# A transformer block's late modulation sums: half parts, a ring of three weight buffers, and Pool's queue

## The chip, the cores and the metric

The kernel runs on one core of a Trainium2 chip. The core has five engines that work side by side, each through its own instructions in a fixed order: TensorE (PE, with its weight loads shown as PEld), VectorE (DVE), ScalarE (ACT), GpSimd (POOL) and SyncE (SP), which only issues transfers. [...] The metric is the device time of one execution in microseconds (us), lower being better. All data is float32.

## The reference, cut to what matters

One layer of a hybrid diffusion block over 1024 tokens of width 1024, with 256 context tokens. A vector `c` gives six modulation vectors: `mod = silu(c) @ w_ada + b_ada`, split into shift, scale and gate for the mixers (parts 0, 1, 2) and for the feed-forward part (3, 4, 5).

```python
mod = jax.nn.silu(c) @ w_ada[i] + b_ada[i]
sh1, sc1, g1, sh2, sc2, g2 = jnp.split(mod[:, None, :], N_MOD, axis=-1)
h = modulate(rmsnorm(x, norm1_g[i]), sh1, sc1)
q, k, v, hv, hx1, hx2, gna, ghy = jnp.split(h @ w_in[i], IN_SPLITS, axis=-1)
y_na = neighbourhood_attention(q, k, v, k_c, v_c, na_rpb[i])    # with 256 context keys
y_hy = hyena_mixer(hv, hx1, hx2, *hy_params)
x = x + g1 * gated_merge(gna, ghy, y_na, y_hy, w_na_o[i], w_hy_o[i], w_out[i])
h2 = modulate(rmsnorm(x, norm2_g[i]), sh2, sc2)
x = x + g2 * swiglu(h2, ffn_w1[i], ffn_w3[i], ffn_w2[i])
return rmsnorm(x, final_g)
```

The Hyena mixer convolves over all tokens with long filters. A filter is a small network of the position (64 hidden units, then `w3`) times an exponential decay, and the convolution is done by Fourier transforms: `irfft(rfft(u) * rfft(filter))`, for two orders and 512 channels. The filters depend on parameters only, not on `x`.

## The kernel before, in words

**Stages.** After the first norm the kernel holds the modulated tokens (`hT`, split into two halves of precision, `hTh` and `hTl`) in SBUF. `project` multiplies them by 40 column chunks of `w_in`, three matrix products for each pair of tiles (`in_ps`, L194); chunks 4 to 11 also multiply the context (`ctx_ps`). Results are evacuated from PSUM by ScalarE (`proj`), for some chunks turned to token order on TensorE (`tm_ps`) and copied by ScalarE (`tm`, L554, two buffers, one PSUM bank `psc`), and stored to scratch memory by DMAs on Pool's queue (`qk`, `kc`, `vtok`, `vctok`, `z`, `hx`, L555, L606 and L618). The weights of the next chunk are loaded on SP (`wr`, L180) and split by ScalarE (`wh`) and VectorE (`wl`).

**Beside the projection** runs the generator `side()`: first the filters' spectra merged with the late modulation's sums, then four convolutions (order 0 and 1, each for two halves of the channels). `_merged` sets the order of the program: it draws from each generator by the units that it yields against its weight, filters 97 and sums 39, and `side` 460 against 39 chunks of projection. The program order decides the order on every engine; the framework below adds the semaphores.

**`filters`** (L335 on) works in four blocks, one for each order and half of the channels. In a block, TensorE computes 8 tiles of raw filter (`filt_ps`, L349), VectorE multiplies each by its decay tile `dec` (L353, result `fv`), which SP loads (L346) into two buffers. Then VectorE does three levels of butterflies (`fx`, `x`, `b`, `a`, L361 to L413), and TensorE multiplies the 8 results `a` by transform matrices `matf`, loaded on SP (`dft_ps`, L425 to L427). ScalarE copies each `dft_ps` to `ks` (L372, three buffers), and SP stores it to scratch memory as a spectrum (L373), which a convolution reads later (L453). `filt_ps` and `dft_ps` share a ring of five PSUM banks, `psf`.

**`ada_sums`** (L843 on) computes modulation parts 2 to 5 without TensorE. For each part VectorE clears an accumulator of 128 x 1024 (`aacc`, L848), SP copies the bias into its first row (L849), and in eight steps SP loads 128 rows of `w_ada` (`wal`, 512 KB, L852) and VectorE adds them, each row times its element of `silu(c)` (L853). `wal` and `aacc` have one buffer each. The accumulator is stored to scratch memory on Pool's queue (L855). Much later `ada_late` (L857 on) reads the four accumulators and adds their 128 rows up on TensorE.

**The pool** `filt` that holds these tiles is closed when filters and sums are done, and the convolutions' tiles take its place in SBUF.

Of the kernel before, what the change touches and what calls it, by code (L numbers as in the profile page):

```python
# [10 lines left out]
F32 = mybir.dt.float32  # L11
F32R = mybir.dt.float32r
AF = mybir.ActivationFunctionType
ALU = mybir.AluOpType
# [4 lines left out]
P = 128  # L19
D = 1024  # L20
# [138 lines left out]
class Block:  # L159
# [176 lines left out]
    def filters(self, pool, psf, hid, w3):  # L336

        nc, a = self.nc, self.a
        for hf in range(2):
            for o in range(2):  # L340
                v = [pool.tile([P, 4, 2, 256], F32, tag="v8", name="fv") for _ in range(2)]
                c0 = o * 512 + hf * 256
                for n2 in range(0, 8, 2):
                    for j in range(2):
                        dec = pool.tile([P, 512], F32, tag="dec", name="dec", bufs=2)
                        nc.sync.dma_start(dec, a["decay"][hf, n2 // 2, j])  # L346
                        ps = psf.tile([P, 512], F32, tag="f", name="filt_ps")
                        for n in range(2):
                            nc.tensor.matmul(ps[:, n * 256:(n + 1) * 256],  # L349
                                             hid[64 * j:64 * j + 64, (n2 + n) * P:(n2 + n + 1) * P],  # L350
                                             w3[64 * j:64 * j + 64, c0:c0 + 256], start=True, stop=True)
                        i = n2 % 4
                        nc.vector.tensor_tensor(v[n2 // 4][:, i:i + 2, j, :], ps.rearrange("p (n c) -> p n c", n=2),  # L353
                                                dec.rearrange("p (n c) -> p n c", n=2), op=ALU.mult)
                    yield 1.3
                b = pool.tile([1, 256], F32, tag="hb", name="hb", bufs=1)
                nc.sync.dma_start(b, a["hbias"][0:1, o, hf, :])
                nc.vector.scalar_tensor_tensor(v[0][0:1, 0, 0, :], b, 2.0 ** -10, v[0][0:1, 0, 0, :],
                                               op0=ALU.mult, op1=ALU.add)
                x = pool.tile([P, 4, 2, 256], F32, tag="v8", name="fx")  # L360
                nc.vector.tensor_add(x[:, :, 0, :], v[1][:, :, 0, :], v[1][:, :, 1, :])  # L361
                nc.vector.tensor_sub(x[:, :, 1, :], v[1][:, :, 1, :], v[1][:, :, 0, :])
                fl = lambda t: t.rearrange("p a b c -> p (a b c)")
                nc.vector.scalar_tensor_tensor(fl(v[1]), fl(x), S2, fl(v[0]), op0=ALU.mult, op1=ALU.add)
                yield 4.6
                nc.vector.scalar_tensor_tensor(fl(x), fl(x), -S2, fl(v[0]), op0=ALU.mult, op1=ALU.add)
                parts, spectra = self.forward(pool, psf, v[1], x)
                for ci in range(5):
                    if ci:
                        for j, us in enumerate(spectra()):  # L370
                            k = pool.tile([P, 512], F32, tag="ks", name="ks", bufs=3)
                            nc.scalar.copy(k, us)  # L372
                            nc.sync.dma_start(self.spec[o][hf][ci - 1][j], k)  # L373
                    if ci < 4:
                        parts()
                        yield 5.4 if ci % 2 == 0 else 1.9
# [466 lines left out]
    def ada_sums(self, pool):  # L843

        nc, a = self.nc, self.a
        for part in range(2, 6):
            acc = pool.tile([P, D], F32, tag="aacc", name="aacc", bufs=1)
            nc.vector.memset(acc, 0.0)  # L848
            nc.sync.dma_start(acc[0:1, :], a["b_ada"][0:1, part * D:(part + 1) * D])  # L849
            for k in range(8):  # L850
                w = pool.tile([P, D], F32, tag="wal", name="wal", bufs=1)
                nc.sync.dma_start(w, a["w_ada"][k, :, part * D:(part + 1) * D])  # L852
                nc.vector.scalar_tensor_tensor(acc, w, self.cs[:, 2 * k:2 * k + 1], acc, op0=ALU.mult, op1=ALU.add)  # L853
                yield 1.2
            nc.gpsimd.dma_start(self.accd[part], acc)  # L855

    def ada_late(self, pool, psf, gates):  # L857

# [578 lines left out]
```

## Time and profile before

| | |
|---|---|
| device time, median of 3 runs (lowest to highest) | 1757.57 us (1751.41 to 1759.25) |
| profiled execution: device time | 1752.59 us |
| profiled execution: span from first to last instruction | 1750.7 us |
| mean granted TensorE clock | 0.981 |
| TensorE busy | 1670.1 us (95% of the span) |
| VectorE busy | 1226.4 us (70%) |
| ScalarE busy | 662.8 us (38%) |
| Pool busy | 142.8 us (8%) |
| moved by DMA | 285.36 MB, 163 GB/s over the span |

The profile is one execution. A row of a group gives line, engine, operation, result and operands, count, busy time and mean duration, then idle time of the engine just before and what ended it ("<-" and the releaser). A row of waits gives who waited for whom: us in total, times, the longest. SPq is SP's DMA queue. A row of DMA issues gives the count, the size and the median time from issue to landing. In a row of a stretch stand its bounds and length, the busy time of each engine in the order PE, PEld, DVE, ACT, POOL (count of instructions in brackets), then the granted TensorE clock (1.00 is full), the DMA engines' mean busy share and GB/s.

### The profile page before, as it was taken

Reading aid. Unit: us, or ns where it says so; the run is one execution under the profiler, and the core shown is the slowest. Engines: PE = TensorE matmul, PEld = TensorE weight load, DVE = VectorE, ACT = ScalarE, POOL = GpSimd, SP = SyncE. Lnnn points to the kernel's source line nnn. Section 1 sums busy time; section 2 is a strip of 40 time slices with the busy share of each in tenths; the row PEclk is TensorE's granted clock in tenths of the full one; section 3 lists DMA queues with packets and bytes.
Section 4 is the critical chain, followed back from the end, with each engine's and each line's share of the span. In section 5 each row is a group of like instructions: output and inputs, shape, how many; then the busy total and the mean of one; then the engine's idle time right before and its main releaser. Section 6 shows DMA issues by size and latency. Waiting matters only on the chain.

```text
span 1750.7 us, 22516 instructions
## 1 busy us (share of the span) xinstructions
PE 1670.1 (95%) x8128; PEld 1324.1 (76%) x8128; DVE 1226.4 (70%) x2039; ACT 662.8 (38%) x1147; POOL 142.8 (8%) x250
## 2 busy tenths in 40 slices
PE   5999899999999998999998999999999999999997
PEld 2777676777777776787777787788888888878886
DVE  4586487799797865656865868887665656479467
ACT  4611222313221213546664215633343333344555
POOL 0000110101000004010300000001000001100000
PEclk8999999999999999999999999999999999999999
DMA  8375766655464428436757424243322322394344
GB/s 337 112 244 189 242 197 211 210 155 181 137 210 155 173 81 238 129 119 190 204 164 253 146 67 168 106 142 133 108 91 102 103 97 97 126 381 149 102 120 151
DMA packets 111469, 285.36 MB, mean 163 GB/s; under 512 B 14707, under 2 KB 23543, under 8 KB 109053
## 3 DMA queue, kind: packets, MB, share of 16 engines
q1 hardware_dynamic: 91888, 221.32, 38.6%
q0 software_dynamic: 18816, 62.14, 10.4%
q8 instruction: 65, 1.06, 0.3%
q10 hardware_dynamic: 653, 0.44, 0.1%
q14 instruction: 47, 0.39, 0.1%
HBM read 213.86 MB, written 69.99 MB: 162 GB/s over the span
## 4 chain that ended last, share of the span: by engine, by line
PE 50%; issue 27%; DVE 9%; DMA 9%; POOL 3%; ACT 2%; SPq 0%; POOLq 0%; DVEq 0%; ACTq 0%
PE in_ps L194 17%; PE dx_ps L1306 6%; PE out_ps L1086 5%; PE dft_ps L425 4%; PE dz_ps L1306 3%; DMA wal<-in_w_ada 2%; PE dft_ps L426 2%; PE dft_ps L427 2%; PE x_ps L1148 2%; PE dy_ps L1306 2%; POOL g L1259 1%; PE pt_ps L761 1%; PE na_ps L194 1%; DVE aacc L853 1%; DMA kraw<-qk 1%
## 5 line engine op out<-in xcount | busy, mean ns | idle before, releaser
L194 PE MATMUL in_ps<-hTh,wl 128*128 128x512 f32 x640 | 258.8, 405 | 6.4 <-ACT proj L596 6.2
L194 PE MATMUL in_ps<-hTh,wh 128*128 128x512 f32 x640 | 252.6, 395 | 0.0
L194 PE MATMUL in_ps<-hTl,wh 128*128 128x512 f32 x640 | 252.5, 395 | 0.0
L194 PEld LDWEIGHTS in_ps<-hTh,wl 128*128 128x128 f32 x640 | 121.5, 190 | 34.2 <-ACT proj L596 6.8
L194 PEld LDWEIGHTS in_ps<-hTh,wh 128*128 128x128 f32 x640 | 121.5, 190 | 26.4 <-issue 0.7
L194 PEld LDWEIGHTS in_ps<-hTl,wh 128*128 128x128 f32 x640 | 121.8, 190 | 25.6 <-issue 1.3
L175 DVE TENSOR_TENSOR ol<-ws,oh 128x512 fp32r<-128x512 f32 x88 | 60.2, 689 | 56.7 <-ACT oh L174 56.5
L174 ACT CAST wh<-wr 128x1024 fp32r<-128x1024 f32 x40 | 41.9, 1048 | 126.7 <-PE in_ps L194 102.5
L175 DVE TENSOR_TENSOR wl<-wr,wh 128x1024 fp32r<-128x1024 f32 x40 | 48.8, 1220 | 55.9 <-ACT wh L174 55.8
L175 DVE TENSOR_TENSOR ol<-ar,oh 128x512 fp32r<-128x512 f32 x77 | 53.0, 688 | 46.4 <-ACT oh L174 46.4
L174 ACT CAST oh<-ar 128x512 fp32r<-128x512 f32 x77 | 47.9, 621 | 82.5 <-PE dx_ps L1306 37.1
L425 PE MATMUL dft_ps<-a,matf 128*128 128x512 f32 x128 | 69.0, 622 | 9.1 <-DVE a L413 5.5
L174 ACT CAST oh<-ws 128x512 fp32r<-128x512 f32 x88 | 54.3, 622 | 48.4 <-PE x_ps L1148 16.8
L1306 PE MATMUL dx_ps<-ol,oh 128*128 128x512 f32 x176 | 69.7, 396 | 1.7 <-DVE ol L175 1.7
L1306 PE MATMUL dx_ps<-oh,ol 128*128 128x512 f32 x176 | 67.5, 392 | 3.9 <-ACT oh L174 3.6
L749 DVE CUSTOM_DVE_ANT_0 pe<-s_ps,bias 128x640 f32<-128x640 f32 x64 | 50.1, 820 | 29.1 <-PE s_ps L744 29.1
L750 ACT ACTIVATE pe<-pe,mx 128x640 f32<-128x640 f32 x64 | 52.6, 822 | 44.8 <-DVE mx L749 44.7
L1306 PE MATMUL dx_ps<-oh 128*128 128x512 f32 x176 | 69.3, 394 | 0.0
L853 DVE SCALAR_TENSOR_TENSOR aacc<-wal,cs,aacc 128x1024 f32<-128x1024 f32 x32 | 41.1, 1283 | 39.7 <-DMA wal<-in_w_ada 39.5
L175 DVE TENSOR_TENSOR ol<-wr,oh 128x512 fp32r<-128x512 f32 x70 | 48.1, 689 | 20.0 <-ACT oh L174 19.9
L174 ACT CAST oh<-wr 128x512 fp32r<-128x512 f32 x70 | 43.2, 621 | 50.0 <-PE y_ps L1148 18.2
L1088 DVE TENSOR_TENSOR x<-x,out_ps 128x512 f32<-128x512 f32 x64 | 43.2, 685 | 21.5 <-PE out_ps L1086 21.5
(392 smaller groups left out, 4234.2 us busy)
## 6 DMA issues: line engine op xcount, KB each, us to landing
wr<-in_w SPq DMA_DIRECT2D x50, 512.0 KB, 3.3
wr<-in_w_in SPq DMA_DIRECT2D x40, 512.0 KB, 4.5
ar<-g SPq DMA_DIRECT2D x77, 256.0 KB, 2.7
wal<-in_w_ada SPq DMA_DIRECT2D x32, 512.0 KB, 4.0
g<-t POOLq DMA_DIRECT2D x49, 256.0 KB, 3.0
matf<-in_dft_f SPq DMA_DIRECT2D x32, 384.0 KB, 4.6
bias<-in_rpb SPq DMA_DIRECT2D x64, 192.0 KB, 3.0
w<-in_w SPq DMA_DIRECT2D x44, 256.0 KB, 5.4
```

The source lines that it names most:

```text
L174: self.nc.scalar.copy(hi, src)
L175: self.nc.vector.tensor_sub(lo, src, hi.bitcast(F32))
L194: mm = nc.tensor.matmul(ps, ww[:, k * P:(k + 1) * P], xx[:, k, pos:pos + width], start=(i == 0), stop=(i == n - 1))
L425: nc.tensor.matmul(ps, m[:, 0], v.rearrange("p a b -> p (a b)"), start=True, stop=False)
L426: nc.tensor.matmul(ps[:, 0:256], m[:, 1], v[:, 1], start=False, stop=False)
L427: nc.tensor.matmul(ps[:, 256:512], m[:, 2], v[:, 0], start=False, stop=True)
L749: nc.vector.tensor_tensor_reduce(pe, ps[:, 256:896], bt, -1.0, 3e38, ALU.add, ALU.min, mx[:, 0:1])
L750: nc.scalar.activation(pe, pe, AF.Exp, bias=mx[:, 0:1], scale=-1.0, accum_out=mx[:, 1:2])
L853: nc.vector.scalar_tensor_tensor(acc, w, self.cs[:, 2 * k:2 * k + 1], acc, op0=ALU.mult, op1=ALU.add)
L1086: nc.tensor.matmul(ps, gg[x][:, tk], ww[y][:, sl], start=(i == 0), stop=(i == n - 1))
L1088: nc.vector.tensor_add(x1[:, sl], x1[:, sl], ps)
L1306: nc.tensor.matmul(ps[j], x[u][:, j * P:(j + 1) * P], w[v], start=(start and i == 0 and c == 0), stop=(stop and i == N - 1 and k == len(re ...
```

## The change

`ada_sums` is rewritten. The 4 parts x 8 steps become 4 parts x 2 halves x 8 steps, on tiles of 128 x 512. The weights are loaded by DMAs on Pool's queue, 256 KB each, into a ring of three buffers; the load of step n + 2 is written ahead of the sum of step n. The accumulator has two buffers; it is cleared by Pool in place of VectorE, and its bias row is copied on Pool's queue. Each half is stored on its own, on Pool's queue as before. A step yields 0.6 in place of 1.2, so that the sums weigh the same in the merge. Besides, the stores of the spectra move from SP's to Pool's queue, and the decay tiles have four buffers in place of two. The arithmetic is the same.

```diff
--- before.py
+++ after.py
@@ -342,7 +342,7 @@
                 c0 = o * 512 + hf * 256
                 for n2 in range(0, 8, 2):
                     for j in range(2):
-                        dec = pool.tile([P, 512], F32, tag="dec", name="dec", bufs=2)
+                        dec = pool.tile([P, 512], F32, tag="dec", name="dec", bufs=4)
                         nc.sync.dma_start(dec, a["decay"][hf, n2 // 2, j])
                         ps = psf.tile([P, 512], F32, tag="f", name="filt_ps")
                         for n in range(2):
@@ -370,7 +370,7 @@
                         for j, us in enumerate(spectra()):
                             k = pool.tile([P, 512], F32, tag="ks", name="ks", bufs=3)
                             nc.scalar.copy(k, us)
-                            nc.sync.dma_start(self.spec[o][hf][ci - 1][j], k)
+                            nc.gpsimd.dma_start(self.spec[o][hf][ci - 1][j], k)
                     if ci < 4:
                         parts()
                         yield 5.4 if ci % 2 == 0 else 1.9
@@ -843,16 +843,27 @@
     def ada_sums(self, pool):
 
         nc, a = self.nc, self.a
-        for part in range(2, 6):
-            acc = pool.tile([P, D], F32, tag="aacc", name="aacc", bufs=1)
-            nc.vector.memset(acc, 0.0)
-            nc.sync.dma_start(acc[0:1, :], a["b_ada"][0:1, part * D:(part + 1) * D])
-            for k in range(8):
-                w = pool.tile([P, D], F32, tag="wal", name="wal", bufs=1)
-                nc.sync.dma_start(w, a["w_ada"][k, :, part * D:(part + 1) * D])
-                nc.vector.scalar_tensor_tensor(acc, w, self.cs[:, 2 * k:2 * k + 1], acc, op0=ALU.mult, op1=ALU.add)
-                yield 1.2
-            nc.gpsimd.dma_start(self.accd[part], acc)
+        steps = [(part, h, k) for part in range(2, 6) for h in range(2) for k in range(8)]
+        cols = lambda part, h: slice(part * D + h * 512, part * D + h * 512 + 512)
+        ws = []
+
+        def load(part, h, k):
+            ws.append(pool.tile([P, 512], F32, tag="wal", name="wal", bufs=3))
+            nc.gpsimd.dma_start(ws[-1], a["w_ada"][k, :, cols(part, h)])
+
+        for step in steps[:2]:
+            load(*step)
+        for n, (part, h, k) in enumerate(steps):
+            if n + 2 < len(steps):
+                load(*steps[n + 2])
+            if k == 0:
+                acc = pool.tile([P, 512], F32, tag="aacc", name="aacc", bufs=2)
+                nc.gpsimd.memset(acc, 0.0)
+                nc.gpsimd.dma_start(acc[0:1, :], a["b_ada"][0:1, cols(part, h)])
+            nc.vector.scalar_tensor_tensor(acc, ws.pop(0), self.cs[:, 2 * k:2 * k + 1], acc, op0=ALU.mult, op1=ALU.add)
+            if k == 7:
+                nc.gpsimd.dma_start(self.accd[part][:, h * 512:(h + 1) * 512], acc)
+            yield 0.6
 
     def ada_late(self, pool, psf, gates):
```

## The prediction

> **What bounds the kernel now.** I read the page's busy times first, then busy time by stretch, to find the stage that the edited lines belong to.
>
> ```profile
> PE 1670.1 (95%) x8128; PEld 1324.1 (76%) x8128; DVE 1226.4 (70%) x2039; ACT 662.8 (38%) x1147; POOL 142.8 (8%) x250
> ```
> ```profile
> core 0: us, PE busy (x) PEld busy (x) DVE busy (x) ACT busy (x) POOL busy (x), PEclk, DMA share, GB/s
> 77.00:340.00 263.00, 245.90 (x1122) 188.60 (x1121) 180.68 (x229) 59.33 (x96) 20.39 (x30) 0.95 0.65 210
> 400.00:650.00 250.00, 249.56 (x1050) 191.98 (x1049) 202.23 (x339) 53.70 (x76) 15.03 (x24) 1.00 0.47 159
> ```
>
> TensorE is the bound: 95% of the span, and 249.56 of 250 us in the convolutions at 400 to 650. All edited code runs in the filter stage, 77 to 340 us. There TensorE idles 263.00 - 245.90 = 17.1 us, and its clock is 0.95 where the convolutions have 1.00. Those are full, so a microsecond won here reaches the end of the kernel. The idle time, from the timeline of TensorE, with the wait and its releaser in brackets:
>
> ```profile
> 120.26 1.10 PE L425 MATMUL dft_ps<-a,matf 128*128 128x512 f32 x2 [2.64 <-issue]
> 143.50 2.07 PE L349 MATMUL filt_ps<-fw,hid 64*128 64x256 f32 x4 [2.28 <-DVE fv L353]
> 172.44 1.10 PE L425 MATMUL dft_ps<-a,matf 128*128 128x512 f32 x2 [0.96 <-issue]
> 201.68 2.08 PE L425 MATMUL dft_ps<-a,matf 128*128 128x512 f32 x2 [3.14 <-DVE a L413]
> 215.37 1.13 PE L349 MATMUL filt_ps<-fw,hid 64*128 64x256 f32 x4 [1.99 <-DVE fv L353]
> 245.01 1.22 PE L425 MATMUL dft_ps<-a,matf 128*128 128x512 f32 x1 [1.72 <-DVE a L413]
> 281.08 2.07 PE L349 MATMUL filt_ps<-fw,hid 64*128 64x256 f32 x4 [3.65 <-DVE fv L353]
> ```
>
> Seven waits, 16.4 us, all before a matrix product whose operand (`a`, in the two rows that name only "issue" too) or whose freed PSUM bank (`fv`) comes from VectorE. After them the clock falls (stretches of 5 us; the granted clock stands before the DMA share):
>
> ```profile
> 140.00:145.00 5.00, 2.72 (x9) 1.83 (x8) 2.65 (x4) 0.00 (x0) 0.00 (x0) 0.76 0.92 313
> 145.00:150.00 5.00, 5.00 (x14) 3.58 (x13) 2.48 (x3) 0.59 (x1) 0.00 (x0) 0.56 0.62 198
> 200.00:205.00 5.00, 3.32 (x6) 2.02 (x7) 3.42 (x4) 0.20 (x1) 0.71 (x1) 0.56 0.77 219
> 205.00:210.00 5.00, 5.00 (x24) 3.33 (x23) 1.95 (x2) 1.17 (x2) 0.00 (x0) 0.75 0.86 307
> 245.00:250.00 5.00, 4.99 (x14) 3.09 (x15) 4.33 (x8) 1.07 (x2) 0.38 (x2) 0.66 0.51 159
> 280.00:285.00 5.00, 3.92 (x9) 2.70 (x10) 3.69 (x5) 0.00 (x0) 0.00 (x0) 0.50 0.65 215
> ```
>
> Busy time times what the clock lacks of 1 gives 0.65 + 2.2 + 1.46 + 1.25 + 1.70 + 1.96 = 9.2 us of work at a lowered clock that full speed would not have needed. The prize is therefore 16.4 + 9.2 = 26 us at most. [...] By a reading that counts idle time alone the prize would be 16.4.
>
> Why is VectorE late, when it is busy only 180.68 of 263 us? Its own waits in this stage:
>
> ```profile
> DVE aacc L853 <- DMA wal<-in_w_ada: 39.5, 18, 7.4
> DVE aacc L848 <- DMA acc<-aacc: 11.7, 3, 6.3
> DVE fv L353 <- DMA dec<-in_decay: 6.5, 5, 2.9
> ```
>
> 57.7 us, all three at tiles that the change gives more buffers. VectorE works in order, so a sum that waits for its weights holds `fv` and `a` behind it.
>
> **The change part by part.** First, the sum by halves. Before, 32 products over 1024 columns; after, 64 over 512, whose price is that of the 512-column product `a`. Four memsets leave VectorE.
>
> ```profile
> L853 DVE SCALAR_TENSOR_TENSOR aacc<-wal,cs,aacc x32: 1272/1284/1286, 86.8 to 319.1; 128x1024 f32<-128x1024 f32 x32
> L413 DVE SCALAR_TENSOR_TENSOR a<-x,b 128x512 f32<-128x512 f32 x32 | 21.5, 686 | 4.6 <-PE dft_ps L427 4.5
> L848 DVE MEMSET aacc<- 128x1024 f32 x4 | 3.6, 912 | 12.0 <-DMA acc<-aacc 11.7 <-DVE hcTl L175 0.3
> ```
>
> 64 x 0.686 = 43.9 against 32 x 1.284 = 41.1 is +2.8; minus 3.6 for the memsets, VectorE's work changes by -0.8 us: nothing.
>
> Second, the ring. Before, one `wal` buffer: load and sum alternate, and each load starts only when the sum ahead has read the buffer. After, the load of step n+2 is issued ahead of step n's sum and needs the buffer of step n-1. It has two steps to arrive. There are 64 steps between the first sum (86.8) and the last (319.1), so a step is 232 / 64 = 3.6 us and two are 7.2.
>
> ```profile
> wal<-in_w_ada SPq DMA_DIRECT2D x32, 512.0 KB, 4.0
> spec<-ks SPq DMA_DIRECT2D x32, 256.0 KB, 4.1
> g<-t POOLq DMA_DIRECT2D x49, 256.0 KB, 3.0
> hx<-tm POOLq DMA_DIRECT2D x16, 256.0 KB, 4.9
> ```
>
> 256 KB on Pool's queue land in 3.0 to 4.9 us (its own rows, other directions of copy); I take 4.5, since DMA is as busy here as beside `hx`. That leaves 7.2 - 4.5 = 2.7 us of slack, against none before. Bounds: loads always on time, 39.5 us of VectorE's waits go; loads late as often as before, none go.
>
> What that does at one stall, the last and longest, can be followed in VectorE's timeline:
>
> ```profile
> 274.07 0.69 DVE L353 TENSOR_TENSOR fv<-filt_ps,dec 128x512 f32<-128x512 f32 x1 [3.14 <-PE filt_ps L349]
> 275.14 0.67 DVE L353 TENSOR_TENSOR fv<-filt_ps,dec 128x512 f32<-128x512 f32 x1
> 277.36 1.28 DVE L853 SCALAR_TENSOR_TENSOR aacc<-wal,cs,aacc 128x1024 f32<-128x1024 f32 x1 [1.55 <-DMA wal<-in_w_ada]
> 280.33 1.36 DVE L353 TENSOR_TENSOR fv<-filt_ps,dec 128x512 f32<-128x512 f32 x2 [1.69 <-DMA dec<-in_decay]
> ```
>
> The third `fv` frees the bank TensorE waits for. It starts at 280.33; with neither wait it would follow 275.14 + 0.67 + 0.69 for a half sum = 276.5, and TensorE, which stopped at 281.08 - 3.65 = 277.43, would hardly stop. The waits ahead of the others work alike, and each `a` stall stands behind more VectorE waiting than its own 1 to 3 us. So with loads on time nearly all 26 us go.
>
> Third, four decay buffers: they remove the 6.5 us above (0 if the loads are late for another reason: the lower bound). They count in the same 26.
>
> Fourth, the accumulator: two buffers, so a new half need not wait for the store of the one before, 11.7 us of VectorE. But its memset, its bias row and its weights now stand in one queue. At each of the 8 starts Pool issues load n+2 (waiting for sum n-1), then the memset, then the bias copy, and sum n waits for that copy. The nearest prices:
>
> ```profile
> L1253 POOL DMA_DIRECT2D g<-t x27 | 14.6, 541 | 309.4 <-DVE t L1251 283.8 <-DVE ol L175 25.0
> masks.py:197 POOL MEMSET ident<- 128x128 f32 x1 | 0.2, 204 | 0.3 <-POOLq L1433 0.3
> aacc<-in_b_ada SPq DMA_DIRECT2D x4, 4.0 KB
> ```
>
> No row has a Pool memset of 128x512; between 0.2 (128x128) and 0.9 (VectorE's, twice as wide) I take 0.8, four times the first. Then 0.54 + 0.8 + 0.54 + about 2.5 for the landing (no time is shown for it; below the 3.0 of 256 KB, above 0) = 4.4 us after the previous sum, against a step of 3.6: some 1 us of VectorE at 8 places, 0 to 2 each. TensorE's share of VectorE's waits so far is 16.4 of 57.7, so this is worth 8 x 0.3 = 2 us with 0 to 5 as bounds.
>
> Fifth, Pool's queue. It gains 64 weight loads, 8 bias rows, 32 spectra and 4 more stores: 108 x 0.54 = 58 us, and 8 x 0.8 = 6; with 20.4 now it is 85 of 263 us. Time is there; order is the question. A weight load now stands behind stores that wait for ScalarE:
>
> ```profile
> POOL vtok L555 <- ACT tm L554: 88.1, 8, 42.3
> POOL z L555 <- ACT tm L554: 64.4, 8, 27.8
> POOL vctok L555 <- ACT tm L554: 11.3, 4, 5.1
> ACT ks L372 <- PE dft_ps L427: 39.0, 23, 5.3
> SPq L373 <- ACT ks L372: 39.9, 24, 8.8
> SPq L852 <- DVE aacc L853: 36.3, 24, 3.8
> ```
>
> The 39.9 us in which SP stood before spectra now stand in Pool's queue; the copy they wait for comes up to 5.3 us after ScalarE is ready, more than the slack of 2.7. So some sums will still be late. Upper bound: all of the prize; lower bound 0; I take a quarter, 6 us. SP loses what held it, 36.3 us before weight loads and 39.9 before spectra, and its decay, DFT and projection weights come no later than now; no gain is counted for it, because no TensorE wait names them. At the change to the convolution (about 335) the last spectrum's landing, 4.1 on SP, may take up to 4.9 on Pool: 0 to 1 us, and TensorE has projection work there; 1 us.
>
> Sum: 26 - 2 - 6 - 1 = 17 us. Against the profiled execution's 1752.59 that is 1735.6; that execution lies 5 us under the median of the three runs (1757.57), from which it would be 1740.6. I predict the middle, 1738.
>
> **The rivals.** *All of it* (15%): no load late, 26 us: 1752.6 - 26 = 1727. For it: 2.7 us of slack at every step. Against: the 39.9 us of waits now ahead of the loads.
>
> *The stalls only move* (25%): sums are late behind the spectra as often as they were for lack of a buffer, so 5 us at most remain: about 1751. [...] Against, in rows: the waits come from a single buffer and from order, more than from the DMA's share of 0.65.
>
> *Slower through Pool's stores* (18%): a weight load that waits for its ring slot, which is for VectorE, now holds the projection's stores behind it. ScalarE's `tm` copies have two buffers and one PSUM bank; late stores hold ScalarE, and with it the evacuations TensorE needs. In this stage 8 + 4 + 8 token stores go that way. Held half a step each, 20 x 1.8 = 36 us of TensorE; minus the 26, +10: 1763. It decides from a mean hold of 26 / 20 = 1.3 us upward. For it: SP's 36.3 us for the same buffer. Against: with three buffers most of that goes.
>
> **How the numbers follow.** The forecast has 42%, with 1728 to 1747 as its own range. 0.5%, about what a measurement can tell here, is 8.8 us: faster is below 1748.8, slower above 1766.4. Faster: 0.40 of the forecast, all of the first rival, a quarter of the second: 0.61. Slower: most of the tail of the third, 0.14. Same: 0.25. The range runs from the full prize, a little under it, 1724, to the third rival, 1763.
>
> **What would show it.** In the profile after: waits of the sum for `wal` under 15 us in total instead of 39.5, none of the memset, none for `dec`; the seven TensorE waits at under 5 us in sum; clock 0.98 or more in this stage; the last sum and the start of the first convolution 15 to 20 us earlier; the rest of the span as long as now. Wrong would be: new waits of ScalarE for token stores, Pool's queue standing ahead of `wal` loads for over 3 us often, or a stage that is shorter while the convolutions, with TensorE's waits at their start, grow.

## The result, and the profile after

The changed kernel takes 1766.11 us (median; 1764.7 to 1773.74), the kernel before on the same chip 1757.15 (1751.41 to 1759.25). The ratio is 1.0072 [1.005, 1.0094] (in brackets, here and below, the 95% interval): **slower by 9 us**, where 1738 was forecast. The profiled execution took 1765.8 us with a span of 1764.0 and a clock of 0.977.

Busy time by stretch of the changed kernel (columns as before):

```profile
77.00:340.00 263.00, 238.03 (x1091) 183.01 (x1090) 182.25 (x255) 57.68 (x94) 81.20 (x144) 0.95 0.62 205
400.00:650.00 250.00, 249.47 (x1051) 191.24 (x1049) 200.25 (x336) 56.46 (x80) 16.52 (x26) 1.00 0.47 158
```

The convolutions are as full as before; the filter stage has lost 245.90 - 238.03 = 7.9 us of TensorE. Its last spectrum copy (`ks`) in ScalarE's timeline, first of the kernel before, then of the changed one:

```profile
333.72 0.59 ACT L372 COPY ks<-dft_ps 128x512 f32<-128x512 f32 x1 [0.33 <-PE dft_ps L427]
```
```profile
340.07 0.59 ACT L372 COPY ks<-dft_ps 128x512 f32<-128x512 f32 x1 [0.33 <-PE dft_ps L427]
```

The two profiled executions lie 1765.8 - 1752.59 = 13.2 us apart (that of before is 4.6 us under its own median). Of these, 6.4 are there when the stage ends; the other 6.9 arise in later stages, whose code is the same, and were not followed. From the last `ks` to the end, the profiled executions of all kernels in this document take between 1416.9 and 1428.2 us, so a microsecond at the end of this stage isn't always one at the end of the kernel.

TensorE's larger waits after the change, from its timeline:

```profile
137.90 1.22 PE L349 MATMUL filt_ps<-fw,hid 64*128 64x256 f32 x4 [3.44 <-DVE fv L353]
179.29 1.64 PE L425 MATMUL dft_ps<-a,matf 128*128 128x512 f32 x2 [2.89 <-DVE a L413]
209.71 2.08 PE L425 MATMUL dft_ps<-a,matf 128*128 128x512 f32 x2 [6.52 <-DVE a L413]
223.57 2.67 PE L349 MATMUL filt_ps<-fw,hid 64*128 64x256 f32 x8 [3.76 <-DVE fv L353]
```

The kind is the same as before, VectorE late with `a` or `fv`, and the longest wait has grown from 3.65 to 6.52 us. What VectorE waited for in this stage, at the two tiles with more buffers:

```profile
DVE aacc L863 <- DMA wal<-in_w_ada: 35.2, 21, 4.9
DVE fv L353 <- DMA dec<-in_decay: 10.3, 7, 2.1
```

The sums wait for their weights almost as long as before (39.5), in spite of a ring of three. VectorE's timeline around the longest wait shows why:

```profile
184.73 0.69 DVE L413 SCALAR_TENSOR_TENSOR a<-x,b 128x512 f32<-128x512 f32 x1 [0.98 <-PE dft_ps L427]
190.30 0.75 DVE L863 SCALAR_TENSOR_TENSOR aacc<-wal,cs,aacc 128x512 f32<-128x512 f32 x1 [4.87 <-DMA wal<-in_w_ada]
193.00 0.75 DVE L863 SCALAR_TENSOR_TENSOR aacc<-wal,cs,aacc 128x512 f32<-128x512 f32 x1 [1.95 <-DMA wal<-in_w_ada]
194.22 1.54 DVE L863 SCALAR_TENSOR_TENSOR aacc<-wal,cs,aacc 128x512 f32<-128x512 f32 x2 [0.47 <-DMA wal<-in_w_ada]
198.56 2.33 DVE L863 SCALAR_TENSOR_TENSOR aacc<-wal,cs,aacc 128x512 f32<-128x512 f32 x3 [2.80 <-DMA wal<-in_w_ada]
202.84 1.54 DVE L863 SCALAR_TENSOR_TENSOR aacc<-wal,cs,aacc 128x512 f32<-128x512 f32 x2 [1.96 <-DMA wal<-in_w_ada]
204.71 0.75 DVE L863 SCALAR_TENSOR_TENSOR aacc<-wal,cs,aacc 128x512 f32<-128x512 f32 x1 [0.33 <-DMA wal<-in_w_ada]
207.17 0.75 DVE L863 SCALAR_TENSOR_TENSOR aacc<-wal,cs,aacc 128x512 f32<-128x512 f32 x1 [1.71 <-DMA wal<-in_w_ada]
207.84 1.22 DVE L175 TENSOR_TENSOR wl<-wr,wh 128x1024 fp32r<-128x1024 f32 x1
208.97 0.68 DVE L413 SCALAR_TENSOR_TENSOR a<-x,b 128x512 f32<-128x512 f32 x1
```

Eleven sums in a row, a **train**, stand between two products `a`; TensorE waits 6.52 us for the second. That `a` and the `wl` ahead of it start with no wait of their own behind the last sum, though VectorE stood idle before sums of the train for 14.1 us in all: they stand behind the train until it has passed. In the kernel before, two instructions of the sums stood at the same place:

```profile
191.48 1.28 DVE L853 SCALAR_TENSOR_TENSOR aacc<-wal,cs,aacc 128x1024 f32<-128x1024 f32 x1 [7.39 <-DMA wal<-in_w_ada]
199.04 0.91 DVE L848 MEMSET aacc<- 128x1024 f32 x1 [6.27 <-DMA acc<-aacc]
199.87 1.16 DVE L175 TENSOR_TENSOR wl<-wr,wh 128x1024 fp32r<-128x1024 f32 x1
200.95 0.68 DVE L413 SCALAR_TENSOR_TENSOR a<-x,b 128x512 f32<-128x512 f32 x1
```

The train's sums come every (207.17 - 190.30) / 10 = 1.69 us, not every 0.75. A reason at hand is that a ring of three gives three sums per round trip, from the issue of a load to the sum that reads it. The rows of the group, of the DMA issues (a DMA is a transfer), and of Pool's waits:

```profile
L863 DVE SCALAR_TENSOR_TENSOR aacc<-wal,cs,aacc x64: 729/749/753, 87.1 to 255.7; 128x512 f32<-128x512 f32 x64
```
```profile
wal<-in_w_ada POOLq DMA_DIRECT2D x64, 256.0 KB, 3.8
```
```profile
POOL wal L852 <- DVE aacc L863: 65.5, 35, 7.3
POOL spec L373 <- ACT ks L372: 14.1, 9, 2.7
```

3.8 us from issue to landing and 0.75 to be summed are 4.55, by three 1.5; the train shows 1.69. And all 64 sums are done between 87.1 and 255.7, where the 32 of before were spread to 319.1: they have been drawn forward and bunched. Pool's loads wait 65.5 us for sums and its spectra only 14.1 for ScalarE: the ring is short of free slots, and spectra hold it little.

By its units and weights the program hands out a sum for every 0.6 x 97 / 39 = 1.5 of the filters' units: about one sum after a unit of 1.3, three or four after one of 4.6 or 5.4. VectorE ran eleven in a row. So the framework orders each engine's instructions anew, as the experiment on the order confirms, and my sentence that the program's order decides was wrong. The order is made ahead of the chip: for two kernels below the expectation names trains of sixteen and of fourteen before the run, the trace shows just these, and one call in the program changes the order. (The kernel uses that call, `keep_in_program_order`, elsewhere, as at L197.) *Trains theory*: the new order bunches the sums, and the ring's round trip sets the pace of each bunch. *Rival*: Pool's queue, where stores stand ahead of the loads.

### The profile page after: what moved, and what is told of

Read it like the earlier page. It is cut to its first block, busy times and chain, and to the rows that moved or that the text cites. A ratio compares the mean times of both kernels' runs of the same rounds, so it can differ in the third digit from the quotient of the medians.

```text
span 1764.0 us, 22658 instructions
## 1 busy us (share of the span) xinstructions
PE 1676.5 (95%) x8128; PEld 1328.9 (75%) x8128; DVE 1228.4 (70%) x2067; ACT 662.6 (38%) x1147; POOL 204.5 (12%) x366
## 4 chain that ended last, share of the span: by engine, by line
PE 51%; issue 29%; DMA 8%; DVE 5%; POOL 4%; ACT 2%; SPq 0%; POOLq 0%; ACTq 0%; DVEq 0%
PE in_ps L194 17%; PE dx_ps L1317 6%; PE out_ps L1097 5%; PE dft_ps L425 4%; PE dz_ps L1317 3%; PE x_ps L1159 2%; DMA wal<-in_w_ada 2%; PE dft_ps L427 2%; PE dft_ps L426 2%; PE dy_ps L1317 2%; PE na_ps L194 1%; PE pt_ps L761 1%; PE hy_ps L194 1%; POOL g L1270 1%; PE pt_ps L775 1%
## 5 line engine op out<-in xcount | busy, mean ns | idle before, releaser
L863 DVE SCALAR_TENSOR_TENSOR aacc<-wal,cs,aacc 128x512 f32<-128x512 f32 x64 | 47.7, 746 | 36.5 <-DMA wal<-in_w_ada 35.2
```

Source lines behind the costliest of these rows:

```text
L863: nc.vector.scalar_tensor_tensor(acc, ws.pop(0), self.cs[:, 2 * k:2 * k + 1], acc, op0=ALU.mult, op1=ALU.add)
```

## The experiments

Kernels were compared on several chips, always beside the kernel before on the same one, whose median came out between 1753.37 and 1757.15 us; across them the ratios are what to compare.

**One part at a time, on the kernel before.** Only the new `ada_sums`; only the spectra moved; only the decay tiles changed.

```diff
-                            nc.sync.dma_start(self.spec[o][hf][ci - 1][j], k)
+                            nc.gpsimd.dma_start(self.spec[o][hf][ci - 1][j], k)
```
```diff
-                        dec = pool.tile([P, 512], F32, tag="dec", name="dec", bufs=2)
+                        dec = pool.tile([P, 512], F32, tag="dec", name="dec", bufs=4)
```

> The kernel before with only the new sums (half parts, ring of three on Pool's queue); spectra stay on SP's queue, two decay buffers. Trains theory (the planner, which sees loads arrive early, puts up to 12 sums in a row ahead of the products that TensorE waits for, and a train runs at the pace of its loads): the loss is all here, 1764 to 1770, TensorE waiting 6 us or more before one matrix product near 200 us. Pool's stores theory (loads late behind the spectra's stores): without the spectra on Pool the loss is gone, 1745 to 1757.

> The kernel before with only the spectra's stores moved to Pool's queue. Trains theory: the order of the sums hardly changes, so the time stays within 4 us of 1757. Pool's stores theory: nothing stands behind the stores on Pool but other stores, so also 1757; it tells whether the move costs by itself (over 1761) or saves (under 1753).

> The kernel before with only four decay buffers. The prediction gave these 6.5 us of VectorE's waits, a ninth of 26 us of TensorE's: 1752 to 1757. Trains theory: any early operand changes the order too; sums still alternate with their single buffer, so no train is possible, 1750 to 1760.

The sums alone: 1782.73 us against 1754.37, 1.0158 [1.0127, 1.0189]. The spectra alone: 1757.42, 1.0032 [1.0013, 1.0052]. The decay buffers alone: 1758.07, 1.0021 [1.0007, 1.0036]. VectorE's waits with the sums alone, and TensorE's longest:

```profile
DVE aacc L863 <- DMA wal<-in_w_ada: 41.6, 27, 5.1
DVE fv L353 <- DMA dec<-in_decay: 13.8, 8, 3.1
```
```profile
220.71 2.08 PE L425 MATMUL dft_ps<-a,matf 128*128 128x512 f32 x2 [8.96 <-DVE a L413]
```

All of the loss sits in the rewritten sums, where no spectrum stood on Pool's queue, and it is larger than the trains theory gave; the other two parts win back over half of it when they are put beside it.

**The order.** The changed kernel, with each sum kept where the program has it, and the same done to the kernel before.

```diff
-            nc.vector.scalar_tensor_tensor(acc, ws.pop(0), self.cs[:, 2 * k:2 * k + 1], acc, op0=ALU.mult, op1=ALU.add)
+            self.tc.keep_in_program_order(nc.vector.scalar_tensor_tensor(
+                acc, ws.pop(0), self.cs[:, 2 * k:2 * k + 1], acc, op0=ALU.mult, op1=ALU.add))
```

> The changed kernel with each sum kept on VectorE behind what the program writes ahead of it, so that the planner can't draw sums forward into trains (longest 5 in a row, not 11). Trains theory: the wait of 6.5 us near 210 us goes, 1745 to 1757. Pool's stores theory: loads stand behind the same stores, so it stays at 1763 to 1770.

> The kernel before with its sums (one buffer, whole parts, SP's queue) kept in the program's order on VectorE. If the gain of the kernel with sums in order comes from the ring: no gain here, each sum still waits for its load, 1752 to 1762. If it comes from the order alone: about 1741.

The changed kernel in order takes 1741.31 us, 0.9939 [0.9916, 0.9962] of before, lower than the trains theory gave: **the sign turns with the order alone**. Its stretch, its waits of VectorE and its last `ks`:

```profile
77.00:340.00 263.00, 251.62 (x1187) 196.01 (x1187) 193.94 (x277) 65.40 (x105) 84.16 (x148) 0.98 0.68 228
```
```profile
DVE fv L353 <- DMA dec<-in_decay: 12.1, 11, 3.0
DVE aacc L863 <- DMA wal<-in_w_ada: 10.9, 7, 3.6
```
```profile
320.21 0.59 ACT L372 COPY ks<-dft_ps 128x512 f32<-128x512 f32 x1 [0.33 <-PE dft_ps L427]
```

TensorE is busy 13.6 us more between 77 and 340 us than in the changed kernel, the sums' waits fall from 35.2 to 10.9, and the stage ends 19.9 us earlier. The expectation names five sums for the longest train; between 195 and 230 us VectorE's timeline shows no more than two sums in a row. It is VectorE's order that tells the two kernels apart: of TensorE's first 2000 matrix products, which reach beyond 470 us, 1980 come in the same sequence in both, and of ScalarE's first 330 instructions 329. (Between the kernel before and the changed one, 1701 of the 2000 do: the change moved TensorE's order too, but the faster kernel has nearly the same new order as the slower one.) The kernel before in order takes 1766.13, 1.0057 [1.0033, 1.0081], above both ranges: with one weight buffer, keeping the order does harm. Order and ring are needed together.

**The pace of a train.** The order is left free, but 62 of the 64 weight loads are left out, so that the sums read the first two tiles again and again and never wait for weights.

```diff
-            ws.append(pool.tile([P, 512], F32, tag="wal", name="wal", bufs=3))
-            nc.gpsimd.dma_start(ws[-1], a["w_ada"][k, :, cols(part, h)])
+            if len(held) < 2:
+                held.append(pool.tile([P, 512], F32, tag="wal%d" % len(held), name="wal", bufs=1))
+                nc.gpsimd.dma_start(held[-1], a["w_ada"][k, :, cols(part, h)])
+            ws.append(held[k % 2])
```

> The changed kernel, but only two weight tiles are ever loaded and the 64 sums read them in turn: it leaves out 62 of the 64 weight loads, so the late modulation is another. The planner still draws sums forward, in trains up to 16. Trains theory, the part that the ring sets the pace of a train: with nothing to wait for a sum takes 0.75 us, so the wait of TensorE near 210 us falls from 6.5 to under 3 us and the time to 1738 to 1748. Rival, that the moved order alone is at fault (sums ahead of the products, loads or not): 1757 to 1766. Pool's stores theory: no loads behind stores, also about 1740.

1747.1 us, 0.9962 [0.9935, 0.9988]. VectorE and then TensorE at the same place:

```profile
185.09 11.19 DVE L865 SCALAR_TENSOR_TENSOR aacc<-wal,cs,aacc 128x512 f32<-128x512 f32 x16 [6.88 <-DMA aacc<-in_b_ada]
196.20 1.22 DVE L175 TENSOR_TENSOR wl<-wr,wh 128x1024 fp32r<-128x1024 f32 x1
197.33 1.29 DVE L413 SCALAR_TENSOR_TENSOR a<-x,b 128x512 f32<-128x512 f32 x2
```
```profile
198.07 1.12 PE L425 MATMUL dft_ps<-a,matf 128*128 128x512 f32 x2 [2.12 <-DVE a L413]
```

The train is sixteen long now, yet it passes at 11.19 / 16 = 0.70 us each, and TensorE waits 2.12 us instead of 6.52. The 6.88 us ahead of it are a wait for a bias row, not for weights. With it the train keeps VectorE from the next `a` for 6.88 + 11.19 = 18.1 us; in the changed kernel it was 4.87 us and then 17.62 from the first sum to the end of the last, 22.5. The difference, 4.4 us, is that of TensorE's two waits. So a long train without waits for weights costs little, and at the pace of the ring it costs the loss. (The transfers left out also take load off the DMA engines, which are busy 0.48 of the time between 77 and 340 us here and 0.62 in the changed kernel, so this run's gain is an upper bound for that.)

**Pool's queue.** The changed kernel with its spectra back on SP; then with the weights of the sums on SP. The order is free in both.

```diff
-                            nc.gpsimd.dma_start(self.spec[o][hf][ci - 1][j], k)
+                            nc.sync.dma_start(self.spec[o][hf][ci - 1][j], k)
```
```diff
-            nc.gpsimd.dma_start(ws[-1], a["w_ada"][k, :, cols(part, h)])
+            nc.sync.dma_start(ws[-1], a["w_ada"][k, :, cols(part, h)])
```

> The changed kernel with the spectra's stores back on SP's queue; TensorE's order is the same as in the changed kernel and VectorE's trains are 12 and 6 long. Trains theory: no better than the changed kernel, 1762 to 1770. Pool's stores theory: the loads no longer stand behind stores that wait for ScalarE, 1745 to 1757.

> The changed kernel with the weights of the sums loaded on SP's queue; nothing is pinned, so VectorE's order still has trains (one of fourteen sums ahead of an `a`). In the changed kernel three loads ahead of the train of eleven stood on Pool's queue behind the token store `vctok`, which waited 4.3 us for ScalarE's `tm`. If that queue makes the train late, the first wait of the train (4.9 us) goes, TensorE's wait at the `a` behind it falls from 6.5 to about 2 us, and the time is 1752 to 1760. Trains theory: the train's pace is the round trip of a ring of three whatever the queue, so TensorE still waits 4 to 8 us at the `a` behind the long train, the last `ks` comes at 335 to 345, and the time is 1760 to 1770.

Spectra on SP: 1763.06, 1.0049 [1.0021, 1.0077]. Loads on SP: 1759.83, 1.0039 [1.0015, 1.0064]. Both intervals overlap that of the changed kernel. The second run answers to Pool's timeline, which does show the rival at work in one place, ahead of the train of eleven, where a load comes behind a store that waited 4.34 us:

```profile
185.28 0.72 POOL L555 DMA_DIRECT2D vctok<-tm  x1 [4.34 <-ACT tm L554]
185.99 0.57 POOL L852 DMA_DIRECT2D wal<-in_w_ada  x1
```

But with the loads on SP, TensorE's wait at that `a` stays:

```profile
207.53 2.08 PE L425 MATMUL dft_ps<-a,matf 128*128 128x512 f32 x2 [6.46 <-DVE a L413]
```

The train is fourteen long there; these are VectorE's rows of its first sum and of its last:

```profile
187.03 0.75 DVE L863 SCALAR_TENSOR_TENSOR aacc<-wal,cs,aacc 128x512 f32<-128x512 f32 x1 [3.69 <-DMA wal<-in_w_ada]
```
```profile
204.98 0.75 DVE L863 SCALAR_TENSOR_TENSOR aacc<-wal,cs,aacc 128x512 f32<-128x512 f32 x1 [0.46 <-DMA wal<-in_w_ada]
```

A sum comes every (204.98 - 187.03) / 13 = 1.4 us, so the train and TensorE's wait behind it are there without Pool's queue too. The time fell to the border of what the two theories gave; of the queue's share in the whole it can be said only that taking the loads off it lies between a loss of 2.5 us and a gain of 14, by the ends of the two intervals.

**What each part gives once the order is kept.** All five are the changed kernel with its sums in program order, and one thing different: spectra on SP; a ring of two, one step ahead; loads on SP; two decay buffers; loads and spectra on SP.

```diff
-            ws.append(pool.tile([P, 512], F32, tag="wal", name="wal", bufs=3))
+            ws.append(pool.tile([P, 512], F32, tag="wal", name="wal", bufs=2))
...
-        for step in steps[:2]:
+        for step in steps[:1]:
...
-            if n + 2 < len(steps):
-                load(*steps[n + 2])
+            if n + 1 < len(steps):
+                load(*steps[n + 1])
```

> The kernel with sums in order, and the spectra's stores back on SP's queue; orders on TensorE and VectorE nearly unchanged. The prediction charged 6 us for loads late behind spectra on Pool: with that, 1733 to 1738. If the loads wait for their ring slot rather than behind stores: within 3 us of 1741.

> The changed kernel with the sums kept in program order, and a ring of two weight tiles with the load one step ahead. Trains theory with the prediction's slack: a set of weights has one step, 3.6 us, to arrive in place of 7.2, and 256 KB land in 3.8 us in the middle and up to 7.8, so half of the sums would wait 0 to 4 us: waits for `wal` 25 to 40 us, TensorE's waits 10 to 18 us in sum, 1750 to 1758. Rival, that order alone does it and the ring's depth means little: 1739 to 1745, as with the ring of three in order.

> The changed kernel with the sums kept in program order, and the weights of the sums loaded on SP's queue as before; the spectra, the bias rows and the accumulator's clearing stay on Pool. If the ring of three in order is what counts and the queue does not, 1738 to 1746, like the kernel in order with its loads on Pool (1741.3). If the move to Pool's queue is needed, because a load on SP holds decay, transform and projection weights behind it while it waits for its ring slot: waits for `dec` over 20 us, TensorE waiting for `matf` or `wh`, and 1748 to 1760.

> The changed kernel with the sums kept in program order, and two decay buffers as before. If the four decay buffers carry a part of the gain, since with the sums out of the way the decay tiles are what `fv` waits for next: waits for `dec` rise from 12 to 15 to 25 us, TensorE's wait before a filter product 2 to 4 us more, and 1745 to 1750. If they carry none (alone they changed the kernel before by 1.0021): 1738 to 1744, waits for `dec` 10 to 14 us.

> The changed kernel with the sums kept in program order, and both the weights of the sums and the spectra on SP's queue as before; only the accumulator's clearing and its bias row stay on Pool. If Pool's queue gives nothing once the order is kept, 1737 to 1745, like the three kernels in order with a ring of three and four decay buffers so far (1738.7 to 1741.3). If SP needs the relief, because decay and transform weights stand behind loads that wait for their slot and behind spectra that wait for ScalarE: waits for `dec` over 20 us and 1748 to 1758.

| sums in program order, and | us | ratio to before | sums wait for `wal`, us | `fv` for `dec`, us |
|---|---|---|---|---|
| nothing else | 1741.31 | 0.9939 [0.9916, 0.9962] | 10.9 | 12.1 |
| spectra on SP | 1738.68 | 0.9897 [0.9843, 0.9951] | 7.4 | 13.4 |
| loads on SP | 1740.74 | 0.991 [0.9892, 0.9928] | 7.0 | 14.4 |
| loads and spectra on SP | 1743.34 | 0.9949 [0.9928, 0.997] | 7.9 | 14.4 |
| ring of two | 1762.53 | 1.0035 [1.0018, 1.0052] | 35.5 | 5.1 |
| two decay buffers | 1758.53 | 1.0022 [1.0003, 1.0042] | 8.8 | 27.4 |

The rows behind the last two, VectorE's waits with the ring of two and with two decay buffers, and TensorE's wait in the latter:

```profile
DVE aacc L863 <- DMA wal<-in_w_ada: 35.5, 21, 4.2
```
```profile
DVE fv L353 <- DMA dec<-in_decay: 27.4, 20, 4.3
```
```profile
214.60 2.07 PE L349 MATMUL filt_ps<-fw,hid 64*128 64x256 f32 x4 [4.48 <-DVE fv L353]
```

Three things follow. The move to Pool's queue gives nothing that these runs can tell: the four kernels with ring and decay buffers lie between 0.9897 and 0.9949, some 9 us, with intervals that overlap or touch, and loads and spectra both on SP, as before the change, is the slowest of the four where each alone is faster. The third slot is needed: 1.0035 against 0.9939 is about 17 us. So are the four decay buffers, which alone gave nothing: 1.0022 against 0.9939 is about 15 us. I had expected 4 to 9 for them at most; the ring of two missed its range upward as well. The parts don't add up; that one stall of VectorE is enough to use up the slack the others win is my reading of it, which no run tests by itself.

**A deeper ring, order free.** Five weight tiles, loads four steps ahead; two decay buffers, so that five and two tiles take the room of three and four.

```diff
-                        dec = pool.tile([P, 512], F32, tag="dec", name="dec", bufs=4)
+                        dec = pool.tile([P, 512], F32, tag="dec", name="dec", bufs=2)
...
-            ws.append(pool.tile([P, 512], F32, tag="wal", name="wal", bufs=3))
+            ws.append(pool.tile([P, 512], F32, tag="wal", name="wal", bufs=5))
...
-        for step in steps[:2]:
+        for step in steps[:4]:
...
-            if n + 2 < len(steps):
-                load(*steps[n + 2])
+            if n + 4 < len(steps):
+                load(*steps[n + 4])
```

> The changed kernel with a ring of five weight tiles and loads four steps ahead, and two decay buffers in place of four to make room; nothing is pinned. The longest train of sums in VectorE's order is still nine long, ahead of an `a` that TensorE needs. Trains theory: a train of nine finds five sets of weights ready instead of three, so it waits for fewer of them; the waits for `wal` fall from 35 us to 15 to 25, TensorE's wait at that `a` from 6.5 to 3 to 5 us, the last `ks` comes around 332 and the time is 1750 to 1760, between the changed kernel and the one in program order. Rival, that the depth of the ring alone is what lacked: 1738 to 1745 as in program order, waits for `wal` under 12 us. Rival, that the landing on Pool's queue sets the pace whatever the depth: 1762 to 1770, waits for `wal` 35 us or more.

1772.3 us, 1.0097 [1.0067, 1.0127], above all three ranges. VectorE's waits, then five sums of the train of nine, and TensorE at the `a` behind it:

```profile
DVE fv L353 <- DMA dec<-in_decay: 29.6, 17, 6.9
DVE aacc L863 <- DMA wal<-in_w_ada: 18.5, 10, 6.3
```
```profile
201.97 3.90 DVE L863 SCALAR_TENSOR_TENSOR aacc<-wal,cs,aacc 128x512 f32<-128x512 f32 x5 [4.94 <-DMA aacc<-in_b_ada]
```
```profile
209.71 1.12 PE L425 MATMUL dft_ps<-a,matf 128*128 128x512 f32 x2 [1.71 <-DVE a L413]
```

The sums' waits halve, as the trains theory has it, and TensorE waits 1.71 us behind the train where 3 to 5 were expected. Five sums pass in 3.90 us, 0.78 each, once a bias row has come, for which VectorE waits 4.94 us. But the decay tiles, down to two, take the place of the sums' waits. The run shows that the ring's depth bears on the sums' waits, and tells nothing on the time of a deeper ring with four decay buffers.

## Why the prediction was wrong

**The step that failed** is the second part, "It has two steps to arrive", with a step of 232 / 64 = 3.6 us. It spread the 64 sums evenly, which holds only if they stay where the program has them. In the changed kernel they take 255.7 - 87.1 = 168.6 us, bunched, and in the long train a step is 1.69 us: the ring had no slack there, and the "prize" of 26 us was not won but grew. TensorE's idle time and the work lost to a lowered clock, worked out from stretches of 5 us between 80 and 340 us as in the prediction, but over all of them:

| | idle, us | lost to the clock, us | sum |
|---|---|---|---|
| before | 17.1 | 9.9 | 27.0 |
| after | 25.0 | 9.8 | 34.8 |
| after, sums in program order | 11.4 | 4.6 | 16.0 |
| in program order, loads on SP | 8.3 | 1.7 | 10.0 |
| in program order, loads and spectra on SP | 8.0 | 0.0 | 8.0 |
| in program order, two decay buffers | 18.0 | 10.2 | 28.2 |

The changed kernel loses 7.8 us, near the 6.4 by which the stage ends later. In order it wins 11.0, and 17.0 with the loads on SP; by the ratios of their times, 0.9939 and 0.991, these two kernels win 10.7 and 15.8 us, of the 17 that the sum forecast. With loads and spectra both on SP the table has 19.0 but the ratio, 0.9949, only 9.0, so the table doesn't always carry over. The mechanism, a ring that takes sums out of VectorE's way, was right for an order that the kernel did not have.

The prize itself was also too large, at "The waits ahead of the others work alike". With the sums' waits down to 10.9 us, 16.0 of the 27.0 us are still there. The wait ahead of the first `a` is one of them: 2.64 us in the kernel before, 2.58 in the changed one, 2.76 in order. In the changed kernel VectorE is busy for all of the 10.00 us around it (the stretch from 105 to 115 in the last section), so that no ring could take it away.

**The other terms.** *Half sums*: 0.746 us each (group mean), not 0.686; 47.7 in place of 43.9, with no sign on the path. *Decay buffers*: counted inside the 26 as 6.5 us at most; in order they carry about 15 us, and their waits in the changed kernel rose to 10.3. I did not ask what is late next once the sums are not: it is `dec`. *Accumulator start*: Pool's memset took 0.543 us, not 0.8, and VectorE waited 0.9 us in all for a bias row where 8 were allowed; the 2 us were too much. *Pool's queue*: 6 us were taken for loads behind spectra. In the changed kernel spectra held Pool 14.1 us, not 39.9, and taking them away won nothing that can be told. Pool's busy time in the stage, 85 us by the sum, came out at 81.2. *Landing*: 3.8 us where 4.5 was taken. *The last spectrum's* 1 us was not looked at by itself.

**The rivals.** Slower, by Pool's stores that hold ScalarE, had the right sign. The sign that it named did show: ScalarE's waits for the token store `vtok` grew, from the first of these rows (before) to the second (changed).

```profile
ACT tm L554 <- DMA vtok<-tm: 11.0, 3, 5.4
```
```profile
ACT tm L554 <- DMA vtok<-tm: 25.4, 3, 13.1
```

But none of TensorE's waits in this stage of the changed kernel was ended by ScalarE. With the loads off that queue and the order free these waits are still 21.6 us and the kernel is still slower than before; with the sums in order and the loads on Pool they are 10.2. So they too go with the order, and the rival's way was not the one that cost the time. "The stalls only move" came nearest in kind, but named the spectra, not the order, as the cause. That an order could change at all was not among the rivals. The trace of before gave no sign of it at the sums, whose 32 stand singly between other work of VectorE. The program did: it has a call that keeps an instruction in program order.

**What would show it**: waits for `wal` under 15 us (35.2; in order 10.9), none for the memset (none), none for `dec` (10.3; in order 12.1), TensorE's waits under 5 us (25.0 idle; in order 11.4), clock at 0.98 in the stage (0.95; in order 0.98), stage over 15 to 20 us earlier (6.4 later; in order 13.5 earlier). All but the memset failed in the changed kernel. In order, the waits for `wal` and the clock came out as forecast; those for `dec`, TensorE's idle time and the end of the stage did not.

What stays open: why the framework bunched these sums. That it takes an instruction as soon as it thinks its operands are there, and thinks the loads faster than they are, fits the runs but was only argued. That the round trip of the ring sets a train's pace fits 1.69 us in the train of eleven and 0.70 without loads, but no run changed the ring's depth and nothing else with the order free. Nor was it followed why loads and spectra both on SP end the filter stage early (last `ks` at 313) without a kernel as much shorter.

## What to carry to other kernels

Where a framework orders the instructions, read the order of the bound engine's supplier (here VectorE) from the trace before counting on a prefetch distance; where its consumers stand in a row, a prefetch of n steps is worth n times their *shortest* spacing (here two steps of 0.75 us, where the forecast had two of 3.6), and pinning the consumers may be the larger half of the change. Price the parts of a change together: the new sums with their ring, the decay buffers and the order each gave nothing or a loss alone, and about 11 us together. When a stall is taken from an engine whose waits hold up what stands behind them, as VectorE's do here, look which of its other operands has the fewest buffers (here `dec`: 27.4 us of waits with two).

## What the runs showed of the hardware

What a wait costs in clock does not follow its length. In the changed kernel in order, a wait of 2.76 us ahead of this product, and a stretch that starts about there:

```profile
110.81 2.04 PE L425 MATMUL dft_ps<-a,matf 128*128 128x512 f32 x2 [2.76 <-issue]
```
```profile
110.20:117.00 6.80, 6.19 (x11) 3.62 (x12) 4.40 (x8) 0.58 (x1) 3.66 (x7) 0.50 0.55 187
```

Two stretches of the changed kernel, at its waits of 6.52 and 3.76 us:

```profile
207.10:213.90 6.80, 4.19 (x7) 2.32 (x8) 5.25 (x7) 0.00 (x0) 4.12 (x7) 0.50 0.81 248
224.20:230.90 6.70, 6.70 (x18) 4.89 (x17) 4.62 (x8) 0.00 (x0) 1.10 (x3) 0.50 0.86 277
```

All three run at 0.50 for about 6.8 us: the fall after 2.76 us is as deep and as long as those after 3.76 and 6.52. (The 0.56 to 0.76 of the stretches of 5 us in the prediction are means over a part at 1.00 and a part at 0.50: in stretches of half a microsecond the kernel before stands at 1.00 up to 142.5, at 0.50 from 143.0 to 149.0 and at 1.00 from 149.5.) Length doesn't tell either whether the clock falls at all. In the kernel before, a wait of 1.72 us, at 245.01, was enough (1.00 up to 245.0, 0.50 from 245.5 to 248.0); in the changed one, this wait of 2.58 us was not:

```profile
109.83 1.10 PE L425 MATMUL dft_ps<-a,matf 128*128 128x512 f32 x2 [2.58 <-issue]
```
```profile
105.00:115.00 10.00, 7.42 (x28) 5.00 (x28) 10.00 (x17) 1.76 (x3) 5.04 (x10) 1.00 0.71 211
```

What is lost to the clock goes with the number of falls in the stage: four in the kernel before and four in the changed one (9.9 and 9.8 us lost, though the second idles 7.9 us more), two in order (4.6), one with the loads on SP (1.7), none with loads and spectra on SP. What decides whether a wait brings a fall, these runs don't show.
